# A two-layer decoder trunk on one core: the order of scores, softmax and the product with values in differential attention is changed

## The chip, the core and the metric

The kernel runs on one core of a Trainium2 chip. Its time is the device time of one execution in microseconds. A core has five engines that work side by side, each through its own queue in the order written: TensorE (PE; its weight loads are PEld) multiplies, VectorE (DVE) and ScalarE (ACT) do the element-wise work, GpSimd (POOL) does some of it and issues some DMAs, SyncE (SP) issues most DMAs. An instruction waits at the head of its queue until what it needs has been signalled; everything behind it in that queue waits too.

## The reference

Two layers on x of 512 x 1024 (float32). Layer 0 mixes tokens by causal multi-scale pooling, layer 1 by causal differential attention; each is followed by a SwiGLU FFN, and after each of the four parts stands a LayerNorm on `ALPHA * x + part(x)`. The change lies in the attention of layer 1:

```python
q, k, v = split(x @ w_qkv)              # 8 heads; q, k: 2 components of 64; v: 128 wide
for qb in range(4):                     # blocks of 128 query rows
    s = q[:, :, :, q0:kend] . k[:, :, :, :kend] * sm_scale
    p = softmax(where(rel >= 0, s + bias, -inf))
    a = p[:, :, 0] - lam * p[:, :, 1]
    o = a . v[:, :, :kend]
o = o * rsqrt(mean(o * o) + LN_EPS) * subln_g * (1 - lambda_init)
return concat(o) @ w_o
```

## The kernel before

All products are made at nearly float32 precision from pairs of a high and a low half: `split` (line 116) makes the high half by a cast on ACT and the low half by a subtraction on DVE (or on POOL, where `low` says so), and `mm3` (147) adds three matmuls, high by high, high by low and low by high. A 128 x 512 matmul result is one of eight banks, which are handed out in turn as they come free.

Weights come in rows of 128 x 1024 from one array, `wall`. `fetch` loads a row through SP into one of five raw buffers; `ready(upto)` (126) divides rows up to that number into one of six pairs of buffers, and so its place in the program is the place of that work in the queues of ACT and DVE. Rows in the set `by_dma` (105) are divided in another way: ACT writes the high half and a negated copy, and a DMA that POOL issues adds the row itself to the negated high half while it loads it a second time from memory. In attention the rows are counted from `attn`: rows 0 to 7 are for values and head 0's q and k, rows 8 and 9 q and k of head 1 (in the trace the tiles w76 and w77), 10 and 11 the last part of the values (w78, w79), 12 to 23 q and k of heads 2 to 7 (w80 to w91), and from 24 on the rows of `w_o` (w92 to w99).

The order of every queue is the order in which the program is written (`manual_schedule`, 282). `attention` (1000) first makes the values by a Strassen-like scheme with seven products, whose last but one (Q5) goes to two banks named vc; the last (Q3) is added to them in head 1. Then it goes through the heads (loop at 1330). In turn h stand:

- `combine(h - 1, 3)`, `split_values(h - 1)` (vh on ACT, vl on DVE), in turns 1 to 4 an `affine` of the residual (two passes of DVE), and the load of the next bias
- q of head h (24 matmuls), its division, `root(h - 2)` (two matmuls named ss that sum the squares of the head before the last over 128 rows, then a logarithm and an exponential on ACT), k of head h (24 matmuls), `scaled(h - 2)` (a product on DVE, a cast on ACT, a subtraction on DVE), and the division of k; between them `ready` for coming rows
- `transposed(h - 1)`: ten transposes of the combined map of the head before and its division into ah and al (three casts, three subtractions)
- `score_block(h, q)` for the four blocks of query rows: twelve, pairwise concurrent, half-height matmuls for two components, then per component on DVE the addition of the bias with the minimum in one pass (line 1149) and on ACT the exponential with its sum (1154)
- `combine(h, q)` (1159): three operations of DVE that join the two components of a block; blocks 0, 1 and 2 stand behind softmax blocks 1, 2 and 3, block 3 in the next turn
- `mix(h - 1)` (1188), behind block 3: the product o of the values with the map of the head before (twelve matmuls), its square on ACT (1203), and the division of the square into sqh (ACT) and sql (POOL; in the last head DVE)

Behind the loop `gather` multiplies by the rows of `w_o`, in two parts of four heads. Between the third and the fourth row of its first step stands `root` of head 6, later `transposed`, `mix` and `root` of head 7. In turn 7 `ready` divides w92 and w93 around q and k, w94 behind the transposes and w95 behind score block 0.

Of the kernel before, what the change touches and what calls it, by code (L numbers as in the profile page):

```python
# [16 lines left out]
ALU = mybir.AluOpType  # L17

P = 128
# [7 lines left out]
HEADS = 8  # L27
# [27 lines left out]
def trunk(ctx, tc, x, wall, pscale, lam_p, subln, table, lng, lnb, band, first, onehot, out):  # L55
# [38 lines left out]
    attn = 2 + 3 * FB  # L94
# [7 lines left out]
    rows_of_wall = list(range(total))  # L102
    rows_of_wall[attn : attn + 24] = order_of_rows
    added = {attn + 6 + r: vrow[1] + r for r in range(2)}
    by_dma = {attn + c for c in (8, 9, *range(12, 24))}

    def fetch(upto):
        while fetched[0] < min(upto, total):
# [891 lines left out]
    def attention():  # L1000
        n = 2
        with tc.tile_pool(name="attn", bufs=1) as ap:
# [55 lines left out]
            where = [base[0]]  # L1058
# [3 lines left out]
                where[0] += count  # L1062
                return [weights(c + i) for i in range(count)]

            vs, qk, soft, outs, mid, biases = {}, {}, {}, {}, {}, {}

            def values(p, r, accs, w):
                wh, wl = w
# [14 lines left out]
            def part(half, side, s):  # L1083
                return vals[:, 2 * half + s, side * 512 : (side + 1) * 512]
# [46 lines left out]
                w1 = ap.tile([P, 4], F32, tag="w1", name=f"w1_{h}", bufs=2)  # L1131
                mid[h] = (mn, sm, w1)

            def score_block(h, q):
                (qh, ql), (kh, kl) = qk[h, "q"], qk[h, "k"]
                mn, sm, _ = mid[h]
                w = (q + 1) * P
                wide = max(w, 256)
                accs = [bank(f"s{h}_{q}_{c}") for c in range(2)]
                qs = slice(q * P, (q + 1) * P)  # L1140
                for i, (a, b) in enumerate(((qh, kh), (qh, kl), (ql, kh))):
                    for c in range(2):
                        r = slice(c * HD, (c + 1) * HD)
                        nc.tensor.matmul(  # L1144
                            accs[c][:, :wide], a[r, qs], b[r, :wide], start=i == 0, stop=i == 2
                        )
                for c in range(2):
                    p = soft[h][c][:, OFF[q] : OFF[q] + w]
                    nc.vector.tensor_tensor_reduce(  # L1149
                        out=p, in0=accs[c][:, :w], in1=biases[h][:, w - 1 :: -1] if w < S else biases[h][:, ::-1],  # L1150
                        op0=ALU.add, op1=ALU.min, scale=1.0, scalar=3.0e38,
                        accum_out=mn[:, q, c : c + 1],
                    )
                    nc.scalar.activation(  # L1154
                        p, p, AF.Exp, bias=mn[:, q, c : c + 1], scale=-1.0,
                        accum_out=sm[:, q, c : c + 1],
                    )
# [96 lines left out]
            def combined(t, a, b, op):  # L1254
                nc.vector.tensor_tensor(t, a, b, op=op)
# [9 lines left out]
            w = take(2)  # L1265
# [7 lines left out]
            w = take(2)  # L1273
# [9 lines left out]
            w = take(2)  # L1283
# [37 lines left out]
            ready(where[0] + 2)  # L1321
            for r in range(2):
                values("Q5", r, vc, w[r])
            for s in range(2):
                combined(part(1, 1, s), vc[s], part(1, 1, s), ALU.subtract)
            ah, al = (ap.tile([P, AW], F32R, tag=t, name=t) for t in ("ah", "al"))
            for t in (ah, al):
                nc.gpsimd.memset(t[:, :P].bitcast(F32), 0.0)

            for h in range(HEADS):  # L1330
                if h > 0:
                    combine(h - 1, 3)
                if h > 0:
                    split_values(h - 1)
                if h == 0:
                    scalars()
                if 0 < h <= SB:
                    affine(n - 1, h - 1)
                if h == SB + 1:
                    load_gb(n)  # L1340
                if h + 1 < HEADS:
                    load_bias(h + 1)
                if h > 0:
                    accs = [bank(f"{nm}{h}") for nm in "qk"]
                    w = take(2)
                    ready(where[0] + (3 if h == 1 else 1))
                    query(accs[0], w[0])
                    split_query(h, "q", accs[0])
                    if h > 1:
                        root(h - 2)  # L1350
                    query(accs[1], w[1])
                    ready(where[0] + (4 if h == 1 else 2))
                    if h > 1:
                        scaled(h - 2)
                    split_query(h, "k", accs[1])
                    if h == 1:
                        w = take(2)
                        for r in range(2):
                            values("Q3", r, vc, w[r])
                        for s in range(2):  # L1360
                            combined(part(0, 1, s), vc[s], part(0, 1, s), ALU.subtract)
                    transposed(h - 1)
                if h == HEADS - 1:
                    ready(where[0] + 3)
                start_scores(h)
                score_block(h, 0)
                if h == HEADS - 1:
                    ready(where[0] + 4)
                score_block(h, 1)
                combine(h, 0)  # L1370
                score_block(h, 2)
                combine(h, 1)
                score_block(h, 3)
                if h > 0:
                    mix(h - 1)
                combine(h, 2)
            cw = where[0]
            combine(HEADS - 1, 3)
            split_values(HEADS - 1)
            ws = take(4)  # L1380
            last = HEADS - 1
            between = [
                lambda: root(last - 1), lambda: transposed(last), lambda: mix(last),
                lambda: root(last),
# [137 lines left out]
```

## Time and profile before

| | |
|---|---|
| three runs | 960.09, 962.82, 961.61 us; median 961.61 |
| the profiled execution | 961.99 us, of which the profile's span is 960.1 |
| attention, from the values to the end of `gather` | about 395 to 615 us of the span |
| a turn of the head loop, from the first ss of one head to the next | 18.0 us (454.32 to 472.29) |
| granted PE clock over the span | 0.992 |

In the profile a row of a timeline gives start, duration, engine, line, operation, output and inputs with their shapes, and in brackets the idle time of the engine ahead of it and what ended it. A matmul of 512 columns is shown with about 0.39 us, but matmuls overlap: the distance of two starts counts, about 0.23 us. In a list of waits stand the engine that waited, for whom, the sum in us, the number of times and the longest. A list of stretches gives for each its length, then for PE, PEld, DVE, ACT and POOL the busy time and the instructions, then the granted clock, the busy share of the DMA engines and GB/s.

### The profile page before, as it was taken

Reading aid. Unit: us, or ns where it says so; the run is one execution under the profiler, and the core shown is the slowest. Engines: PE = TensorE matmul, PEld = TensorE weight load, DVE = VectorE, ACT = ScalarE, POOL = GpSimd, SP = SyncE. Lnnn points to the kernel's source line nnn. Section 1 sums busy time; section 2 is a strip of 40 time slices with the busy share of each in tenths; the row PEclk is TensorE's granted clock in tenths of the full one; section 3 lists DMA queues with packets and bytes.
Section 4 is the critical chain, followed back from the end, with each engine's and each line's share of the span. In section 5 each row is a group of like instructions: output and inputs, shape, how many; then the busy total and the mean of one; then the engine's idle time right before and its main releaser. Section 6 shows DMA issues by size and latency. Waiting matters only on the chain.

```text
span 960.1 us, 14943 instructions
## 1 busy us (share of the span) xinstructions
PE 937.1 (98%) x5712; PEld 831.1 (87%) x5712; DVE 793.0 (83%) x1157; ACT 516.3 (54%) x820; POOL 130.2 (14%) x153
## 2 busy tenths in 40 slices
PE   9999999999999999999999979999999999999996
PEld 8898899999988878878777768898899999988885
DVE  8859889999987588877897775879779999988778
ACT  6752445554664278675778753743335555564450
POOL 4121121110002101001212100221211110001101
PEclk9999999999999999999999989999999999999998
DMA  9386988886868996785665522297888886878942
GB/s 245 129 272 211 339 287 251 255 277 201 257 204 283 347 307 191 175 219 143 143 164 132 129 69 83 73 313 213 286 260 245 260 244 215 255 253 277 359 163 89
DMA packets 86182, 211.63 MB, mean 220 GB/s; under 512 B 15156, under 2 KB 26676, under 8 KB 86110
## 3 DMA queue, kind: packets, MB, share of 16 engines
q1 hardware_dynamic: 43420, 117.16, 37.2%
q0 software_dynamic: 18912, 58.73, 24.4%
q10 hardware_dynamic: 23778, 34.78, 10.0%
q8 instruction: 45, 0.74, 0.3%
q14 instruction: 27, 0.22, 0.1%
HBM read 173.93 MB, written 36.72 MB: 219 GB/s over the span
## 4 chain that ended last, share of the span: by engine, by line
PE 71%; issue 10%; DVE 9%; ACT 4%; DMA 3%; POOL 2%; DVEq 0%; ACTq 0%; POOLq 0%
PE A L861 17%; PE P L928 9%; PE C L861 8%; PE B L861 4%; PE Q L928 3%; PE g L151 3%; PE u L151 3%; PE u L150 3%; PE u L149 3%; PE g L150 3%; PE g L149 3%; PE va L1076 2%; DMA r<-tsum 1%; DMA r<-in_wall 1%; PE wo L149 1%
## 5 line engine op out<-in xcount | busy, mean ns | idle before, releaser
L607 DVE TENSOR_TENSOR raw<-raw,raw 128x1024 f32<-128x1024 f32 x56 | 68.3, 1219 | 0.5
L123 ACT CAST xs<-hid 128x512 fp32r<-128x512 f32 (+1 forms) x60 | 34.7, 581 | 24.3 <-DVE hid L775 24.3
L1154 ACT ACTIVATE p<-p,mn 128x128 f32<-128x128 f32 (+3 forms) x64 | 35.4, 554 | 21.6 <-DVE mn L1149 21.6
L124 DVE TENSOR_TENSOR xs<-hid,xs 128x512 fp32r<-128x512 f32 (+1 forms) x60 | 38.4, 641 | 7.8 <-ACT xs L123 7.8
L249 ACT ACTIVATE y<-pt,bT,gT 128x128 f32<-128x128 f32 x80 | 30.1, 456 | 19.4 <-PE pt L235 19.3
L706 POOL DMA_DIRECT2D b<-in_wall x20 | 14.0, 707 | 171.8 <-DMA tsum<-b 118.1
L767 POOL DMA_DIRECT2D xs<-ssum x24 | 17.5, 727 | 140.4 <-PE Q L928 67.4
L199 POOL TENSOR_TENSOR rs<-rs,mhalf 128x1 f32<-128x1 f32 x16 | 12.6, 787 | 153.8 <-DVE rs L198 114.3
L639 DVE TENSOR_TENSOR hid<-sg,u 128x512 f32<-128x512 f32 x16 | 11.0, 686 | 26.1 <-PE u L151 14.1
L706 POOL DMA_DIRECT2D hid<-in_wall x24 | 18.8, 824 | 82.9 <-DMA tsum<-hid 43.9
L743 ACT CAST v<-u 128x512 fp32r<-128x512 f32 x22 | 13.6, 620 | 27.3 <-DVE u L741 27.2
L1149 DVE CUSTOM_DVE_ANT_0 p<-s,bias 128x128 f32<-128x128 f32 (+3 forms) x64 | 28.1, 484 | 0.0
L124 POOL TENSOR_TENSOR sql<-sq,sqh 128x512 fp32r<-128x512 f32 x7 | 11.7, 1675 | 91.5 <-ACT sqh L123 91.5
L124 DVE TENSOR_TENSOR xt<-y,xt 128x512 fp32r<-128x512 f32 x20 | 13.6, 690 | 12.1 <-ACT xt L123 12.1
L190 DVE BATCH_NORM_STATS2 st<-res 128x6 f32<-128x512 f32 x32 | 22.2, 694 | 1.1
L887 ACT ACTIVATE sg<-sg 128x512 f32<-128x512 f32 x14 | 8.9, 633 | 25.7 <-DVE sg L880 25.7
L707 POOL DMA_DIRECT2D hid<-in_wall x12 | 14.8, 1234 | 53.7 <-DMA hid<-in_wall 47.0
L655 ACT CAST xs<-hid 128x1024 fp32r<-128x1024 f32 x8 | 8.4, 1052 | 24.0 <-DVE hid L672 11.6
L1144 PE MATMUL s<-heads 64*128 64x256 f32 (+2 forms) x168 | 19.9, 349 | 0.0
L876 DVE TENSOR_TENSOR hid<-C,hid 128x512 f32<-128x512 f32 x14 | 9.7, 691 | 10.9 <-PE C L861 9.3
L1168 DVE SCALAR_TENSOR_TENSOR p<-p,sm,p 128x128 f32<-128x128 f32 (+3 forms) x32 | 17.6, 551 | 1.1
L872 ACT COPY hid<-C 128x512 f32<-128x512 f32 x14 | 8.2, 588 | 18.5 <-PE C L861 18.5
(1188 smaller groups left out, 3686.4 us busy)
## 6 DMA issues: line engine op xcount, KB each, us to landing
raw<-in_wall SPq DMA_DIRECT2D x122, 512.0 KB, 4.8
r<-tsum SPq DMA_DIRECT2D x40, 512.0 KB, 4.4
hid<-in_wall POOLq DMA_DIRECT2D x36, 512.0 KB, 6.9
b<-in_wall POOLq DMA_DIRECT2D x30, 512.0 KB, 5.7
r<-in_wall SPq DMA_DIRECT2D x30, 512.0 KB, 4.8
tsum<-hid ACTq DMA_DIRECT2D x24, 512.0 KB, 5.7
ssum<-v ACTq DMA_DIRECT2D x22, 512.0 KB, 3.8
tsum<-b ACTq DMA_DIRECT2D x20, 512.0 KB, 4.8
```

The source lines that it names most:

```text
L123: nc.scalar.copy(dst_h, src)
L124: (low or nc.vector).tensor_tensor(dst_l, src, dst_h.bitcast(F32), op=ALU.subtract)
L149: nc.tensor.matmul(acc, ah, bh, start=start, stop=False)
L150: nc.tensor.matmul(acc, ah, bl, start=False, stop=False)
L151: nc.tensor.matmul(acc, al, bh, start=False, stop=stop)
L249: nc.scalar.activation(y[:, k, :], pt[:, k * P : (k + 1) * P], AF.Identity, bias=bT[:, n, kk : kk + 1], scale=gT[:, n, kk : kk + 1],)
L607: tt(t, raws[pair[0]], raws[pair[1]], op=ALU.add)
L706: nc.gpsimd.dma_start(out=t[:, j], in_=src[:, j])
L861: nc.tensor.matmul(o, w[:, c], x[:, kk, :], start=p in ("P1", "Q5", "P2") and f + kk + e == 0, stop=p in ("Q4", "Q3", "P2") and (f, kk, e) ...
L928: nc.tensor.matmul(accs[s], x[:, k, r], y[:, c], start=first and k == 0 and e == 0, stop=last and k == m - 1 and e == 2, skip_group_check= ...
L1149: nc.vector.tensor_tensor_reduce(out=p, in0=accs[c][:, :w], in1=biases[h][:, w - 1 :: -1] if w < S else biases[h][:, ::-1], op0=ALU.add, o ...
L1154: nc.scalar.activation(p, p, AF.Exp, bias=mn[:, q, c : c + 1], scale=-1.0, accum_out=sm[:, q, c : c + 1],)
```

## The change

- `score_block` is cut in two. `scores` holds the twelve matmuls, with the product of q's low half ahead of that of k's low half; `softmax` holds the work of DVE and ACT.
- In each turn blocks 0 and 1 stay as they are. Then come the scores of blocks 2 and 3, then `mix(h - 1)`, and only then, alternating with `combine` of blocks 0 and 1, softmax blocks 2 and 3. For PE the order of matmuls stays the same (except within a score block), as does DVE's order in turns 1 to 6; on ACT the square and the cast of `mix` now stand ahead of the exponentials of blocks 2 and 3.
- In turn 0 the two subtractions of vc (DVE) move from ahead of the first softmax block to behind the second.
- Row 8 (w76, q of head 1) leaves `by_dma`: DVE makes its low half.
- In turn 7 `ready` divides w92 and w93 ahead of q, and w94 and w95 behind k's matmuls, ahead of `scaled` and the division of k.

```diff
-    by_dma = {attn + c for c in (8, 9, *range(12, 24))}
+    by_dma = {attn + c for c in (9, *range(12, 24))}
...
-            def score_block(h, q):
+            def scores(h, q):
                 (qh, ql), (kh, kl) = qk[h, "q"], qk[h, "k"]
-                mn, sm, _ = mid[h]
-                w = (q + 1) * P
-                wide = max(w, 256)
+                wide = max((q + 1) * P, 256)
                 accs = [bank(f"s{h}_{q}_{c}") for c in range(2)]
                 qs = slice(q * P, (q + 1) * P)
-                for i, (a, b) in enumerate(((qh, kh), (qh, kl), (ql, kh))):
+                for i, (a, b) in enumerate(((qh, kh), (ql, kh), (qh, kl))):
                     for c in range(2):
...
+                maps[h, q] = accs
+
+            def softmax(h, q):
+                mn, sm, _ = mid[h]
+                w = (q + 1) * P
+                accs = maps.pop((h, q))
                 for c in range(2):
                     p = soft[h][c][:, OFF[q] : OFF[q] + w]
...
                 values("Q5", r, vc, w[r])
-            for s in range(2):
-                combined(part(1, 1, s), vc[s], part(1, 1, s), ALU.subtract)
...
+            last = HEADS - 1
             for h in range(HEADS):
...
-                    ready(where[0] + (3 if h == 1 else 1))
+                    ready(where[0] + {1: 3, last: 2}.get(h, 1))
                     query(accs[0], w[0])
...
                     query(accs[1], w[1])
-                    ready(where[0] + (4 if h == 1 else 2))
+                    ready(where[0] + (4 if h in (1, last) else 2))
...
-                if h == HEADS - 1:
-                    ready(where[0] + 3)
                 start_scores(h)
-                score_block(h, 0)
-                if h == HEADS - 1:
-                    ready(where[0] + 4)
-                score_block(h, 1)
-                combine(h, 0)
-                score_block(h, 2)
-                combine(h, 1)
-                score_block(h, 3)
+                for q in range(2):
+                    scores(h, q)
+                    softmax(h, q)
+                if h == 0:
+                    for s in range(2):
+                        combined(part(1, 1, s), vc[s], part(1, 1, s), ALU.subtract)
+                for q in (2, 3):
+                    scores(h, q)
                 if h > 0:
                     mix(h - 1)
+                for q in (2, 3):
+                    combine(h, q - 2)
+                    softmax(h, q)
                 combine(h, 2)
```

More of the change, by code (lines that the diff above doesn't have):

```diff
@@ L1063, in take @@
                 return [weights(c + i) for i in range(count)]
-            vs, qk, soft, outs, mid, biases = {}, {}, {}, {}, {}, {}
+            vs, qk, soft, outs, mid, biases, maps = {}, {}, {}, {}, {}, {}, {}
             def values(p, r, accs, w):
@@ L1380, in attention @@
             ws = take(4)
-            last = HEADS - 1
             between = [
```

## The prediction

> **What bounds the kernel now.** I read the page's first part, then busy time in stretches, then the list of waits between 395 and 600 us (the attention layer), and last the timelines of the engines around the waits that PE shows.
>
> ```profile
> PE 937.1 (98%) x5712; PEld 831.1 (87%) x5712; DVE 793.0 (83%) x1157; ACT 516.3 (54%) x820; POOL 130.2 (14%) x153
> ```
> ```profile
> 415.00:444.00 29.00, 27.23 (x130) 21.59 (x128) 17.61 (x45) 18.22 (x33) 3.79 (x6) 0.94 0.87 230
> 560.00:590.00 30.00, 25.46 (x109) 20.40 (x108) 17.22 (x33) 12.36 (x25) 1.66 (x1) 0.89 0.15 52
> 620.00:700.00 80.00, 80.00 (x434) 69.69 (x433) 64.53 (x73) 33.09 (x45) 15.61 (x18) 1.00 0.86 270
> ```
> ```profile
> PEld ss L1211 <- POOL sql L124: 6.2, 7, 1.5
> PE ss L1211 <- POOL sql L124: 3.1, 7, 0.9
> PE ss L1210 <- ACT sqh L123: 3.6, 1, 3.6
> ```
>
> PE is the bound: 98% busy, and 80.00 of 80 us in the FFN behind the attention layer. So time that PE loses inside the attention layer is lost at the end, and time won there arrives at the end. The stretches (after length: PE, PEld, DVE, ACT, POOL, then granted clock) show two places where PE idles and the clock falls: 415 to 444 (0.94) and 560 to 590 (4.5 us idle, 0.89). The waits name the second and a third: `root`'s two matmuls (ss) wait for the squares of seven heads. What sits in the first stands in part 3.
>
> **The change, part by part.**
>
> *1. The last `root` that stands behind softmax.* Timelines of PE, ACT and POOL at the last head:
>
> ```profile
> 557.52 0.28 PE L151 MATMUL o<-ah,vl 128*128 128x256 f32 x1
> 561.51 0.39 PE L151 MATMUL wo<-w94h,heads 128*128 128x512 f32 x1
> 565.49 0.79 PE L1210 MATMUL ss<-sqh,ones 128*128 128x512 f32 x1 [3.59 <-ACT sqh L123]
> 567.24 0.79 PE L1211 MATMUL ss<-sql,ones 128*128 128x512 f32 x1 [0.95 <-POOL sql L124]
> 567.83 0.63 PE L149 MATMUL wo<-w95h,heads 128*128 128x512 f32 x1
> 572.06 0.41 PE L150 MATMUL wo<-w93l,heads 128*128 128x512 f32 x1
> ```
> ```profile
> 564.22 0.57 ACT L1203 ACTIVATE sq<-o 128x512 f32<-128x512 f32 x1
> 564.82 0.62 ACT L123 CAST sqh<-sq 128x512 fp32r<-128x512 f32 x1
> ```
>
> The product o of head 6 is complete at 557.52 + 0.28 = 557.80, but ACT squares it at 564.22, because `mix` stands in its queue behind the exponentials of blocks 1 to 3, and these wait for DVE. Without a wait ss would follow the matmul of 561.51 at 561.74. From there to 572.06, where the pitch is normal again, PE issues 2 ss and 10 wo matmuls: 12 x 0.23 = 2.7 us at full clock (0.23 is the pitch of head 1's k in part 3: 24 matmuls in 5.44 us), against 10.32 us. **7.6 us** are lost, about 5 of them idle and the rest in matmuls at a pitch of 0.43.
>
> With `mix` queued ahead of softmax blocks 2 and 3, ACT squares at once: 0.6 + 0.6 us puts sqh at 559.0, and POOL's 1.68 us puts sql at 560.8. PE comes for it at 561.7: cover of about 1 us, so the whole 7.6 us goes if o does not start later than now (part 4). If sql is late by more than 1 us, the excess comes back one to one. What is late next? `transposed` of head 7 needs the last `combine`. PE would reach it at 561.74 + 26 x 0.23 = 567.7. The last exponential ends today before the square of 564.22, `combine` within 2 us of it, and both come earlier, since the splits of w94 and w95 leave the softmax. It holds.
>
> *2. The six earlier roots* (heads 2 to 7, roots 0 to 5). First and last of six:
>
> ```profile
> 448.69 0.28 PE L151 MATMUL o<-ah,vl 128*128 128x256 f32 x1
> 454.32 0.39 PE L1210 MATMUL ss<-sqh,ones 128*128 128x512 f32 x1
> 455.02 0.50 PE L1211 MATMUL ss<-sql,ones 128*128 128x512 f32 x1 [0.31 <-POOL sql L124]
> 455.36 0.39 PE L149 MATMUL k<-xt,w81h 128*128 128x512 f32 x1
> ...
> 544.49 0.39 PE L1210 MATMUL ss<-sqh,ones 128*128 128x512 f32 x1
> 545.27 0.50 PE L1211 MATMUL ss<-sql,ones 128*128 128x512 f32 x1 [0.39 <-POOL sql L124]
> ```
> ```profile
> 448.41 0.62 ACT L1154 ACTIVATE p<-p,mn 128x384 f32<-128x384 f32 x1 [0.49 <-DVE mn L1149]
> 451.97 0.58 ACT L1203 ACTIVATE sq<-o 128x512 f32<-128x512 f32 x1
> ```
> ```profile
> 453.29 1.68 POOL L124 TENSOR_TENSOR sql<-sq,sqh 128x512 fp32r<-128x512 f32 x1 [17.17 <-ACT sqh L123]
> ```
> ```profile
> 429.94 0.68 DVE L124 TENSOR_TENSOR vl<-vals,vh 128x512 fp32r<-128x512 f32 x1
> ...
> 453.76 1.75 DVE L124 TENSOR_TENSOR vl<-vals,vh 128x512 fp32r<-128x512 f32 x1
> ```
>
> ss to k takes 1.04 us in the first, against 0.46 for two matmuls: 0.6. In the last the second ss comes 0.78 us behind the first, not 0.70: the same or a little more. With `mix` in front, o ends at 448.97, sqh is there at about 450.2 and sql at 451.9, 2.4 us ahead of 454.32. The price lies on ACT and DVE: the exponential of block 2 starts at 450.2 instead of 448.41, block 3's ends at about 452.9 (0.8 later), and `combine` of blocks 2 and 3 ends about 0.7 us later. Two things pay it back. ACT has its squares behind it, so vh starts when it does now. And `vl` stops colliding: it takes 1.75 us where POOL works on sql and 0.68 where it does not. So DVE leaves vl about 0.4 us earlier than today, and no split of q or k is later. Bounds of what the earlier sql can do to DVE are zero and the 1.07 us of that collision, now in `combine`; I take 0.5 and it does not reach PE. Counted: five heads x 0.6 = **3.1 us**; the sixth (head 7) is spent in part 4.
>
> [...]
>
> Scores now take the q low half second and the k low half third. The waits give 1.2 us over six heads to the k low half today. I count nothing (bounds 0 and 1.2): behind the k split DVE still owes three splits of the transposed map before it releases the banks for block 3 and o, and that chain starts no earlier.
>
> *3. Head 0 and head 1.*
>
> ```profile
> 419.03 0.69 DVE L1255 TENSOR_TENSOR vals<-vc,vals 128x512 f32<-128x512 f32 x1 [5.54 <-PE vc L1076]
> 432.94 1.22 DVE L124 TENSOR_TENSOR w78l<-raw,w78h 128x1024 fp32r<-128x1024 f32 x1
> ```
> ```profile
> 422.29 0.70 PE L1144 MATMUL s<-ksq,qsqh 64*128 64x512 f32 x2 [0.51 <-DVE mn L1149]
> 423.39 0.50 PE L149 MATMUL q<-xt,w76h 128*128 128x512 f32 x1
> 425.39 0.79 PE L151 MATMUL q<-xt,w76l 128*128 128x512 f32 x1 [1.26 <-DMA w76l<-in_wall]
> 432.05 0.39 PE L149 MATMUL k<-xt,w77h 128*128 128x512 f32 x1
> 437.49 0.39 PE L1076 MATMUL vc<-w78h,heads 128*128 128x512 f32 x1
> ```
> ```profile
> 425.00:430.00 5.00, 4.61 (x14) 3.67 (x15) 4.78 (x16) 4.17 (x11) 0.00 (x0) 0.66 0.83 181
> ```
> ```profile
> w81l<-in_wall POOLq DMA_DIRECT2D x1, 512.0 KB, 9.5
> ```
>
> q takes 423.39 to 432.05 = 8.66 us, k with the same 24 matmuls 5.44: 3.2 us go to the wait for w76l's landing and to the halved clock behind it (0.66 over 5 us is 1.7 us). With a 1.22 us split on VectorE, in the 5.54 us in which it waits for vc, w76l is there at about 417.7. ACT saves its negated copy (1.06), so w77l's DMA starts 1 us earlier; even with w81l's landing, 9.5 us, the longest in this stretch, it lands about a quarter microsecond before k needs it at 428.3. The two subtractions from vc (2 x 0.69) leave the place ahead of softmax block 0, which then starts about 1 us earlier; block 3 of the scores loses its wait (0.7 us with the restart). They come back behind block 1, so softmax block 2 and everything DVE does after it are 0.2 us later than now. That is the next wait: w78l, done now at 432.94 + 1.22 = 434.16, then at 434.4, while PE reaches it at 433.5. A new stall of 0.9 us. Sum: 3.2 + 0.7 - 0.9 = **3.0 us**.
>
> *4. The wo rows of head 7.*
>
> ```profile
> 549.27 0.75 DVE L1219 SCALAR_TENSOR_TENSOR rso<-o,gcol,rso 128x512 f32<-128x512 f32 x1
> 554.06 1.22 DVE L124 TENSOR_TENSOR w94l<-raw,w94h 128x1024 fp32r<-128x1024 f32 x1
> ```
> ```profile
> 551.24 0.59 ACT L123 CAST heads<-k 128x512 fp32r<-128x512 f32 x1 [0.57 <-PE k L151]
> ```
> ```profile
> 555.64 0.47 PE L149 MATMUL o<-ah,vh 128*128 128x512 f32 x1 [0.55 <-DVE mn L1149]
> ```
>
> w94 and w95 (two casts on ACT, two DVE splits of 1.22) now stand ahead of `scaled`; behind `scaled`'s product wait ACT's cast of it and, in the same queue, the cast of k. Two splits more on DVE (2.4), less what it gains at vl and in idle time (about 1.0), put the product at about 550.7 (549.27 today) and k's cast at 551.9 (551.24), although PE ends k 0.65 us earlier. From k's cast to o the chain loses w94l (1.22 at 554.06), so o starts at 555.5 to 555.6: as now. The head's own 0.6 us is spent, nothing else; PE's idle time moves ahead of the scores. POOL and SP gain no entries there: the raw rows of w92 to w95 are loaded long before.
>
> **Sum**: 7.6 + 3.1 + 3.0 = 13.7 us. The profiled execution took 961.99, so 948.3; the median of the runs is 0.38 lower: **947.9 us**.
>
> **The rivals.** *A stall stays at one of the two halved places.* In head 7 PE idles about 0.9 us ahead of the scores and 1 within them, no less than the two waits (0.51 and 1.26) after which the clock halved in head 1; or w77l lands later than 9.5 us. Either returns 1.7 to 3.2 us: 949.6 to 951.1. For it: both margins are a few tenths. Against: o waits 0.55 us today behind like gaps, and the clock held there.
>
> [...]
>
> *Hidden anyway.* Something behind attention (the first weights of the FFN) ends last, and the gain is given back: about 961.6. Against it: 80.00 of 80 us busy.
>
> [...]
>
> **How the numbers follow.** Forecast 0.67 (945.0 to 949.6: w78l's stall may not come, 0.9, and the k halves may give 1.2, or a lock costs 1 to 1.5); a stall stays 0.22; hidden 0.07; slower 0.04. The range 945.0 to 952.0 holds the first two. This kernel's measurement tells 0.3% (2.9 us) from no change: faster 0.90, within 0.06, slower 0.04.
>
> **What would show it.** Right: in the list of waits ss no longer waits for sqh or sql; the PE timeline runs without a gap from o of head 6 to `root`; the clock column reads 1.00 between 560 and 590 and about 425; q of head 1 takes 5.5 us; a wait of vc for w78l appears. Wrong: PE waiting for the k split in every head, DVE's `combine` stretched by more than 1 us, or a halved window inside head 7.

## The result and the profile after

| | before | after |
|---|---|---|
| runs, us | 960.09, 962.82, 961.61, 961.51 | 948.47, 948.79, 948.29, 950.59 |
| median, us | 961.56 | 948.63 |
| span of the profiled execution, us | 960.1 | 946.7 |
| granted PE clock over the span | 0.992 | 0.997 |

The ratio is 0.987 with an interval of 0.9851 to 0.989. The forecast was 947.9 us, with a range of 945.0 to 952.0: the time lies 0.7 us above the forecast.

The busy times of the changed kernel, from the first part of its page:

```profile
PE 931.2 (98%) x5712; PEld 829.9 (88%) x5712; DVE 787.3 (83%) x1158; ACT 513.8 (54%) x819; POOL 126.5 (13%) x152
```

PE has the same 5712 matmuls and was busy 5.9 us less (937.1 before). So more than half of the 13.4 us by which the span became shorter was idle time of PE, and the rest lay in matmuls that took longer before, many of them under the halved clock: six of q of head 1 and nine of wo took 0.63 us each at a granted clock of 0.50, against 0.39 and 0.40 in the changed kernel at 1.00. The stretches of the changed kernel say where:

```profile
415.00:444.00 29.00, 28.54 (x157) 22.76 (x156) 21.45 (x59) 19.26 (x39) 2.94 (x5) 1.00 0.77 211
547.00:577.00 30.00, 29.82 (x152) 24.86 (x153) 19.64 (x47) 15.19 (x34) 1.29 (x1) 1.00 0.15 52
```

Both places where PE idled are full, and the clock is 1.00 in both (before: 0.94 and 0.89; the second place has moved forward by 13 us). All waits of PE in the attention of the changed kernel (395 to 600 us):

```profile
PE s L1142 <- ACT heads L123: 0.8, 1, 0.8
PE vc L1076 <- DVE w78l L124: 0.5, 1, 0.5
PE s L1142 <- DVE heads L124: 0.3, 1, 0.3
```

The waits of ss for the squares are gone. What is new was forecast: the wait for w78l, and in head 7 two waits of the scores for k.

To count by stage, one reads when PE starts the same matmul in both traces. The start of the first transpose behind attention (pt) and the first scores of heads 0, 1 and 6, before:

```profile
420.28 0.39 PE L1144 MATMUL s<-ksq,qsqh 64*128 64x256 f32 x2
...
444.12 0.39 PE L1144 MATMUL s<-heads 64*128 64x256 f32 x2
...
534.21 0.38 PE L1144 MATMUL s<-heads 64*128 64x256 f32 x2
...
602.22 0.44 PE L235 MATMUL pt<-ident,res 128*128 128x128 f32 x2
```

The same in the changed kernel, with the first o of head 6 ahead of pt:

```profile
420.40 0.39 PE L1142 MATMUL s<-ksq,qsqh 64*128 64x256 f32 x2
...
440.94 0.39 PE L1142 MATMUL s<-heads 64*128 64x256 f32 x2
...
528.05 0.39 PE L1142 MATMUL s<-heads 64*128 64x256 f32 x2
...
549.59 0.51 PE L149 MATMUL o<-ah,vh 128*128 128x512 f32 x1
...
588.62 0.44 PE L235 MATMUL pt<-ident,res 128*128 128x128 f32 x2
```

| stage | won, us | forecast, us |
|---|---|---|
| up to the scores of head 0 | -0.12 | 0 |
| heads 0 and 1, to the scores of head 1 | (444.12 - 420.28) - (440.94 - 420.40) = 3.30 | 3.0 |
| five heads, to the scores of head 6 | (534.21 - 444.12) - (528.05 - 440.94) = 2.98 | 3.1 |
| head 7, to o of head 6 | (555.64 - 534.21) - (549.59 - 528.05) = -0.11 | 0 |
| from there to pt, with the last root | (602.22 - 555.64) - (588.62 - 549.59) = 7.55 | 7.6 |
| sum | 13.60 | 13.7 |

At the end of the span 13.4 of the 13.6 us are left.

### The profile page after: what moved, and what is told of

The parts are those of the page before. It is cut to its first block, busy times and chain, and to the rows that moved or that the text cites. A ratio compares the mean times of both kernels' runs of the same rounds, so it can differ in the third digit from the quotient of the medians.

```text
span 946.7 us, 14942 instructions
## 1 busy us (share of the span) xinstructions
PE 931.2 (98%) x5712; PEld 829.9 (88%) x5712; DVE 787.3 (83%) x1158; ACT 513.8 (54%) x819; POOL 126.5 (13%) x152
## 4 chain that ended last, share of the span: by engine, by line
PE 82%; DVE 9%; ACT 3%; DMA 3%; issue 2%; POOL 0%; DVEq 0%; ACTq 0%; POOLq 0%
PE A L861 17%; PE P L928 9%; PE C L861 9%; PE B L861 4%; PE Q L928 3%; PE g L151 3%; PE u L149 3%; PE u L150 3%; PE u L151 3%; PE g L149 3%; PE g L150 3%; PE va L1076 2%; PE s L1142 2%; DMA r<-tsum 1%; DMA r<-in_wall 1%
## 5 line engine op out<-in xcount | busy, mean ns | idle before, releaser
L743 ACT CAST v<-u 128x512 fp32r<-128x512 f32 x22 | 13.6, 620 | 27.7 <-DVE u L741 27.7
L124 DVE TENSOR_TENSOR xt<-y,xt 128x512 fp32r<-128x512 f32 x20 | 13.6, 690 | 12.1 <-ACT xt L123 12.1
L1142 PEld LDWEIGHTS s<-heads 64*128 64x128 f32 x168 | 14.1, 185 | 5.2 <-issue 1.0
L876 DVE TENSOR_TENSOR hid<-C,hid 128x512 f32<-128x512 f32 x14 | 9.7, 691 | 10.4 <-PE C L861 8.8
```

Of the source, the lines that this page charges most:

```text
L124: (low or nc.vector).tensor_tensor(dst_l, src, dst_h.bitcast(F32), op=ALU.subtract)
L1142: nc.tensor.matmul(accs[c][:, :wide], a[r, qs], b[r, :wide], start=i == 0, stop=i == 2)
```

## The experiments

All kernels here compute the whole reference. "The changed kernel" is the base of each diff, except where the text says otherwise.

The runs were made in several sets, and the median of the kernel before lay between 960.50 and 961.98 us from set to set, so medians of different kernels compare to about 1 us. Therefore the text also counts one stretch in each trace, "scores to pt": from the first scores of head 0 to the first transpose behind attention. It is 602.22 - 420.28 = 181.94 us before and 588.62 - 420.40 = 168.22 in the changed kernel. The scores of head 0 start anywhere from 419.25 to 421.59 us in the thirteen traces, though PE's program up to there is the same in all; the medians hold this scatter, the stretch does not. There is one trace of each kernel.

### Undoing the early squares: e1_squares_last

```diff
                 for q in (2, 3):
                     scores(h, q)
-                if h > 0:
-                    mix(h - 1)
                 for q in (2, 3):
                     combine(h, q - 2)
                     softmax(h, q)
+                if h > 0:
+                    mix(h - 1)
                 combine(h, 2)
```

> The changed kernel, but the product with values and its squares stand behind softmax block 3 again in every turn; all scores still stand ahead, the wo rows, row 8 and the vc subtractions stay as changed. My theory: the wait of ss for sql comes back in heads 2 to 6, 0.6 us each (3.0 us); in head 7 it is absorbed by the late k cast. In the last head sql comes about 8.2 us behind the start of o, PE is there after 6.1: about 2.2 us of wait, and 1.7 us more if the clock halves. So 953.8 us, up to 955.5. Rival A (the order of the squares is worth the whole of parts 1 and 2, the moved wo rows nothing): 948.6 + 10.6 = 959.2. Rival B (the gain came from all scores being queued ahead, not from the squares): 948.6 to 949.5, and no wait of ss in the list.

Measured: 953.99 us (952.87 to 957.13), ratio 0.9936 [0.991, 0.9961]. PE's waits in the attention:

```profile
PE ss L1215 <- POOL sql L124: 3.3, 7, 1.2
```

The last of the seven in the PE timeline:

```profile
560.23 0.50 PE L1214 MATMUL ss<-sqh,ones 128*128 128x512 f32 x1 [0.16 <-ACT sqh L123]
561.97 0.50 PE L1215 MATMUL ss<-sql,ones 128*128 128x512 f32 x1 [1.24 <-POOL sql L124]
```

With the squares behind the exponentials again, PE waits for sql in all seven heads again, and 953.99 - 948.63 = 5.4 of the 10.7 us of parts 1 and 2 are lost (scores to pt: 173.46, 5.2 more than the changed kernel). The last root, however, now costs 1.9 us and not 7.6 (from 559.68 to 562.31 it is 2.63 us for three distances of 0.23: the two waits of 0.16 and 1.24 us and 0.5 us of restarts around them): the rows of `w_o` still stand ahead of head 7's softmax, so the square is late by little. Without early squares the rest of the change thus gives back 5.7 of the 7.6 us. That it is the moved rows is argued, not isolated: they are what the rest changes on DVE and ACT in the last head. That the early squares alone give back nearly all of it is shown by the next two runs.

### Undoing the moved rows of `w_o`: e2_wo_rows_back

```diff
-                    ready(where[0] + {1: 3, last: 2}.get(h, 1))
+                    ready(where[0] + (3 if h == 1 else 1))
...
-                    ready(where[0] + (4 if h in (1, last) else 2))
+                    ready(where[0] + (4 if h == 1 else 2))
...
+                if h == last:
+                    ready(where[0] + 3)
                 start_scores(h)
                 for q in range(2):
+                    if h == last and q == 1:
+                        ready(where[0] + 4)
                     scores(h, q)
```

> The changed kernel, but in head 7 the wo rows are divided in the old places (w94 behind the transposes, w95 between softmax blocks 0 and 1). My theory: k's cast is early again, o starts about 0.6 us earlier than in the changed kernel, w94l and w95l push softmax blocks 0 and 1, so sql comes 0.5 us too late for PE: these cancel, 948.2 to 949.3, with a wait of ss for sql of 0.3 to 0.8 us in the last head and no gap of 1 us ahead of head 7's scores. Rival (most of the last head's 7.6 us came from taking w95 out of the softmax): 951 to 954, with a wait of several us at ss.

Measured: 948.74 us (948.57 to 949.55), ratio 0.9877 [0.986, 0.9895], against 948.63 for the changed kernel. The waits in its attention:

```profile
PE o L149 <- DVE mn L1153: 0.6, 1, 0.6
...
PE ss L1215 <- POOL sql L124: 0.4, 1, 0.4
```

The idle time ahead of head 7's scores is gone; o waits for the softmax as it did before the change, and the last ss waits 0.4 us for sql. It is the same sum in other places (scores to pt: 168.20): beside the early squares the moved rows are worth nothing.

### The early squares alone: e5_squares_alone

The kernel before, with `score_block` cut in two and `mix` ahead of softmax blocks 2 and 3 as in the change; the product of k's low half stays second, and rows 8, w94, w95 and the subtractions of vc stay where they were.

> The kernel before with one part of the change alone: all scores, then the product with values and its squares, then softmax blocks 2 and 3. wo rows, row 8, the vc subtractions and the order of the low halves stay as before. My theory: 3.0 us in heads 2 to 6 and about 7.4 in head 7 and the last root, although w95 still stands in the softmax: 961.6 - 10.4 = 951.2 us. Rival A (the last head needs the wo rows moved too): 955 or more, with a wait of several us at the last ss. Rival B (softmax held up by the squares makes the k split late, which only the other parts hid): 954 or more with PE waiting ahead of the scores in each head.

Measured: 950.82 us (950.52 to 953.37), ratio 0.9906 [0.9881, 0.9931]. By the medians this part carries 10.7 of the 12.9 us. By the trace, against the kernel before, it won 3.0 us in the five heads, 0.6 in head 7 and 6.8 behind it, 10.4 us in all; 1.6 us more were won in heads 0 and 1, which this edit should leave as they were. That is the surprise of this profile: PE waits there and then the stretch from 424 to 434.

```profile
422.74 0.70 PE L1142 MATMUL s<-ksq,qsqh 64*128 64x512 f32 x2 [0.51 <-DVE mn L1153]
425.75 0.50 PE L151 MATMUL q<-xt,w76l 128*128 128x512 f32 x1 [1.17 <-DMA w76l<-in_wall]
```
```profile
424.00:434.00 10.00, 8.83 (x38) 6.96 (x39) 9.71 (x23) 8.67 (x19) 0.64 (x1) 1.00 0.69 168
```

Nearly the same two waits as before (0.51 and 1.26 there), but the granted clock stays at 1.00. The same stretch of the kernel before:

```profile
424.00:434.00 10.00, 8.74 (x32) 6.98 (x32) 9.75 (x22) 8.68 (x18) 0.85 (x1) 0.83 0.66 166
```

So the 1.7 us that part 3 of the prediction puts down to the halved clock at head 1 do not follow from these waits with certainty; in one execution they come, in another not. Before, the clock was halved from 425.23 to 428.64, for 3.41 us, and nearly the whole of both waits lies in the 3.41 us just ahead of that:

```profile
421.82:425.23 3.41, 1.83 (x8) 0.98 (x8) 3.25 (x19) 2.47 (x10) 0.00 (x0) 1.00 1.02 201
425.23:428.64 3.41, 3.25 (x8) 2.58 (x9) 3.30 (x10) 2.58 (x9) 0.00 (x0) 0.50 0.77 192
```

PE was without a matmul for 3.41 - 1.83 = 1.58 us of the first. In e5's trace the two waits add up to 1.68 us, against 1.77 before. Why the clock halved behind the one pair and not behind the other was not shown.

### Undoing the row on VectorE: e3_row8_by_dma and e7_row8_dma_bias_late

```diff
-    by_dma = {attn + c for c in (9, *range(12, 24))}
+    by_dma = {attn + c for c in (8, 9, *range(12, 24))}
```

> The changed kernel, but the low half of head 1's q comes by DMA again. My theory: it lands at about 425.4 us, PE needs it at 423.1: 2.3 us of wait in q of head 1, with 1.7 us more if the clock halves, less the 0.7 us that head 1 now waits for w78l and then no longer does: 950.2 to 951.9 us. Rival (the landing cost little by itself; what won the 3.3 us in heads 0 and 1 was the moved vc subtractions): 948.6 to 949.4.

Measured: 953.99 us (953.75 to 956.12), ratio 0.9935 [0.9915, 0.9956]. That is above the whole expected range: the edit costs 5.4 us (scores to pt: 173.33, 5.1 more). The wait of PE, the landing of w76l and the stretch from 427 on:

```profile
427.26 0.50 PE L151 MATMUL q<-xt,w76l 128*128 128x512 f32 x1 [3.78 <-DMA w76l<-in_wall]
```
```profile
w76l<-in_wall POOLq DMA_DIRECT2D x1, 512.0 KB, 9.2
```
```profile
427.00:432.00 5.00, 4.74 (x14) 3.75 (x15) 4.86 (x12) 4.82 (x9) 0.00 (x0) 0.66 0.71 202
```

Theory and rival had taken w76l's landing from before, 7.6 us. It took 9.2. What had changed beside it is in the SP timelines: the load of head 1's bias, here and (second fence) in the kernel before.

```profile
418.08 0.42 SPq L1117 DMA_DIRECT2D bias<-lines  x1
```
```profile
421.51 0.33 SPq L1117 DMA_DIRECT2D bias<-lines  x1
```

With the subtractions of vc out of the way, the first four small operations of `scalars` run 7.4 us earlier on DVE (from 413.64 here, from 421.00 before); they release a buffer, SP's queue goes on, and the bias is loaded 3.4 us earlier, issued 0.1 us behind w76l (417.97). To test it, the same kernel with that load issued later:

```diff
-                if h + 1 < HEADS:
+                if 1 < h + 1 < HEADS and h != 1:
                     load_bias(h + 1)
...
                     ready(where[0] + {1: 3, last: 2}.get(h, 1))
+                    if h == 1:
+                        load_bias(1)
+                        load_bias(2)
```

> The kernel with row 8 by DMA (e3), but head 1's bias is loaded after the next raw rows instead of as soon as its buffer is free. New theory for the 9.2 us landing of w76l in e3: the moved vc subtractions let the scalars of the lambda term run 3 us earlier, which frees the bias buffer, so that the bias load (issued at 418.1 instead of 421.9) shares the DMA engines with w76l. Then the landing goes back to 7.5 us, the wait in q to about 2.3 us: 952.3 us, or 950.6 where the clock does not halve. [...]

Measured: 952.77 us (951.78 to 954.57), ratio 0.9912 [0.9894, 0.993].

```profile
426.53 0.50 PE L151 MATMUL q<-xt,w76l 128*128 128x512 f32 x1 [2.48 <-DMA w76l<-in_wall]
```
```profile
w76l<-in_wall POOLq DMA_DIRECT2D x1, 512.0 KB, 7.9
```

The landing falls from 9.2 to 7.9 us and the wait from 3.8 to 2.5 (scores to pt: 171.82, 1.5 less than e3), while DVE does the same work in the same order beside it; so the loads made the difference, as far as one landing in each trace can show. The edit moved more than one load: both biases are now issued from 436.22 on, and the next raw row of 512 KB, which stood behind them in SP's queue, came forward from 428.20 to 420.16. That row, 1.6 us behind w76l's issue, may be the 0.3 us left over 7.6; no run here tests it. In these traces the order of DVE's work thus changed, by way of SP's queue, how long a transfer took that DVE neither issues nor reads.

### Undoing the move of the subtractions: e4_vc_back

```diff
+            for s in range(2):
+                combined(part(1, 1, s), vc[s], part(1, 1, s), ALU.subtract)
             ah, al = (...)
...
-                if h == 0:
-                    for s in range(2):
-                        combined(part(1, 1, s), vc[s], part(1, 1, s), ALU.subtract)
```

> The changed kernel, but the two subtractions of vc stand ahead of head 0's first softmax again. My theory: the fourth score block of head 0 waits 0.7 us for its bank again and q of head 1 starts about 0.9 us later; in return PE no longer waits for w78l (0.7 us). The two cancel: 948.7 to 949.1 us. Rival (the moved subtractions win their 0.7 us by themselves, w78l would wait anyway): 949.5 us, with both waits in the trace.

Measured: 948.09 us (947.52 to 948.46), ratio 0.9861 [0.9844, 0.9878]. In its trace the wait for w78l is gone and the wait of the scores for the softmax is back:

```profile
421.83 0.70 PE L1142 MATMUL s<-ksq,qsqh 64*128 64x512 f32 x2 [0.51 <-DVE mn L1153]
```

The move wins about 0.7 us in head 0 and gives it back in head 1. As expected it cancels (scores to pt: 168.40, against 168.22); the run is even 0.5 us below the changed kernel, which these measurements do not tell apart.

### The order within a score block: e6_k_low_second

```diff
-                for i, (a, b) in enumerate(((qh, kh), (ql, kh), (qh, kl))):
+                for i, (a, b) in enumerate(((qh, kh), (qh, kl), (ql, kh))):
```

> The changed kernel, but k's low half is multiplied second again in every score block. My theory: scores to o stays 2.79 us in heads 2 to 6, since block 3 and o wait for the banks that the splits of the transposed map release; 948.6 us, within 0.3. Rival (the third place hides the k split, 0.2 us in each of six heads): 949.8 us and 2.9 to 3.0 us from scores to o.

Measured: 948.23 us (947.79 to 948.82), ratio 0.9863 [0.9849, 0.9878]. By the distances of starts PE again loses 0.26 us per head at k's low half, yet a turn, from the first scores of head 2 to those of head 3, stays at 17.41 us (458.36 to 475.77; in the changed kernel 458.25 to 475.66). What the new order spares at k's low half is lost again before o: from the first scores to o it is 2.80 us here and 2.79 in the changed kernel. That is what the expectation said; that the wait is for banks, as it also said, was not tested. The prediction counted nothing for this edit.

### Better orders: v3_mix_before_scores, v4_affine_in_gaps, v2_order_mended, v5_casts_behind_k

If PE needs an early square, the product with values could stand ahead of all scores. For that the transposes go into the middle of k:

```diff
-                if 0 < h <= SB:
-                    affine(n - 1, h - 1)
...
-                    query(accs[1], w[1])
-                    ready(where[0] + (4 if h in (1, last) else 2))
+                    query(accs[1], w[1], range(KB // 2))
+                    ready(where[0] + (4 if h == 1 else 2))
                     if h > 1:
                         scaled(h - 2)
+                    transposed(h - 1)
+                    if h == last:
+                        ready(where[0] + 3)
+                    if h <= SB:
+                        affine(n - 1, h - 1)
+                    query(accs[1], w[1], range(KB // 2, KB))
                     split_query(h, "k", accs[1])
...
-                    transposed(h - 1)
+                    mix(h - 1)
                 start_scores(h)
...
+                if h == last:
+                    ready(where[0] + 4)
...
-                if h > 0:
-                    mix(h - 1)
```

> A version made from what the traces show to be left: the transposes of the head before stand in the middle of k's matmuls and the product with values directly behind k, ahead of all scores; the affine of the residual stands behind the transposes' splits; in the last head w94 is divided behind the transposes and w95 behind softmax block 1. If the waits left in the scores (for the k split and for the banks of the transposed map) are what costs 0.6 us a head, they go: 7 x 0.6, with 0.7 for w78l and 1.5 in the last head 942.2 us, and PE shows no wait for VectorE or ScalarE between 440 and 545. Rival (VectorE's chain of combine, splits and affine is the next bound, since the transposes now come 5 us earlier): PE waits for combine ahead of the transposes or for the split map ahead of o, 946 us or more.

Measured: 949.0 us (948.34 to 950.69), ratio 0.9874 [0.9856, 0.9891]: a miss, nothing was won over the changed kernel (scores to pt: 169.25, 1.0 more). PE's waits, then DVE around the third of the four:

```profile
PE s L1142 <- DVE heads L124: 4.9, 4, 1.5
```
```profile
492.84 1.61 DVE L124 TENSOR_TENSOR al<-at,ah 128x512 fp32r<-128x512 f32 x3
494.37 1.22 DVE L227 TENSOR_TENSOR res<-res,gb 128x1024 f32<-128x1024 f32 x1
495.62 1.23 DVE L228 TENSOR_TENSOR res<-res,gb 128x1024 f32<-128x1024 f32 x1
496.77 0.68 DVE L124 TENSOR_TENSOR heads<-k,heads 128x512 fp32r<-128x512 f32 x1
```

I had put `affine`, which nobody waits for, between al and the low half of k, for which PE waits. It has 2.45 us in heads 2 to 4, and PE loses 1.7 us in each. The next kernel puts its two halves into gaps of DVE: the first inside `scaled`, ahead of the division, the second behind k's low half (`times` and `plus` are the two lines of `affine`; the base is v3).

```diff
                 nc.vector.scalar_tensor_tensor(rs, acc, gcol, rs, op0=ALU.mult, op1=ALU.mult)
+                if h < SB - 1:
+                    times(n - 1, h + 1)
...
-                    if h <= SB:
-                        affine(n - 1, h - 1)
+                    if h == 1:
+                        affine(n - 1, 0)
...
                     split_query(h, "k", accs[1])
+                    if 1 < h <= SB:
+                        plus(n - 1, h - 1)
```

> The kernel of the last variant (the product with values ahead of the scores), with one thing moved: in turns 2 to 4 the two halves of `affine` (1.22 and 1.23 us on VectorE) no longer stand together ahead of the low half of k. The first stands inside `scaled`, where VectorE waited 1.65 us for the cast of the high half; the second stands behind the low half of k, where VectorE waited about 1.1 us for the first scores in heads 5 to 7. Theory: the order on VectorE alone made TensorE wait 1.68 to 1.70 us ahead of the scores of heads 2, 3 and 4. Then these three gaps go, 3 x 1.69 = 5.1 us, and the run gives 949.0 - 5.1 = 943.9 us (943.2 to 944.8). Rival: the low half of k was late because VectorE's whole turn had become too long, wherever `affine` stands; then the gap is only shared out, at least 1 us per head stays, and the run gives 947 us or more.

Measured: 945.38 us (944.61 to 947.51), ratio 0.9831 [0.98, 0.9861]. The three gaps went. The time is 0.6 us above the expected range, and the waits of PE say why:

```profile
PE o L150 <- DVE al L124: 0.6, 4, 0.2
...
```

Heads 2 to 4 of v3 lost their time ahead of the scores, behind o; now the next heads come to o earlier and wait about 0.3 us (with the restart) for al, as the later heads of v3 did. That gives back 1.0 of the 5.1 us: scores to pt fell by 4.1, to 165.13. The last 0.5 us is within what these runs scatter (2.9 us).

The other way is to leave the change's order and move two pieces: the division of w95 behind softmax block 1 of head 7 (w94 stays ahead of `scaled`; the expectation describes this edit wrongly), and `affine` to just ahead of q's division (in head 1 behind it):

```diff
-                if 0 < h <= SB:
-                    affine(n - 1, h - 1)
...
+                    if 1 < h <= SB:
+                        affine(n - 1, h - 1)
                     split_query(h, "q", accs[0])
+                    if h == 1:
+                        affine(n - 1, 0)
...
-                    ready(where[0] + (4 if h in (1, last) else 2))
+                    ready(where[0] + {1: 4, last: 3}.get(h, 2))
...
+                if h == last:
+                    ready(where[0] + 4)
```

> The changed kernel with three orders altered: the low half of the second row of weights of head 7 behind k instead of ahead of it and the next row's behind softmax block 1 (the PE idle of 0.97 us ahead of head 7's scores should go), `affine` of row 0 behind the split of q in head 1, and `affine` ahead of the split of q in heads 2 to 4. Theory: the idle ahead of head 7's scores (0.97 + 0.50 us) is VectorE's queue, so 1.0 to 1.5 us go, and of head 1's stall (0.62 + 0.11 us) most: 948.6 - 1.0 - 0.6 = 947.0 us (946.3 to 947.8). Rival: the idle only moves to the next wait of the same engine, and the time stays within 0.3% of the changed kernel, 948.1 to 949.1 us.

Measured: 945.76 us (945.34 to 946.13), ratio 0.9827 [0.9803, 0.9851], 0.5 us below the expected range. By the trace the two moves won 2.0 us (scores to pt: 166.22), 0.75 in heads 0 and 1 and 1.1 in head 7, against 1.6 expected; another 1.15 us of its trace lie ahead of the scores of head 0, where nothing was edited. Its list of waits of PE has no entry between 420 and 600 us.

The last kernel is v4 with `ready` for the second row of weights moved behind the division of k:

```diff
-                    ready(where[0] + (4 if h == 1 else 2))
+                    if h == 1:
+                        ready(where[0] + 4)
...
-                    if h == last:
-                        ready(where[0] + 3)
...
                     split_query(h, "k", accs[1])
+                    if h > 1:
+                        ready(where[0] + (3 if h == last else 2))
```

> The kernel of v4_affine_in_gaps with the two casts of the second row of weights (1.03 and 1.06 us on ScalarE) moved from ahead of `scaled` to behind the split of k in turns 2 to 7. Theory: the waits that are left, 0.27 to 0.32 us for the low half of the transposed maps (al) ahead of each product with values from head 1 to head 6, and 0.51 us for k of head 7, come from these casts, behind which ScalarE's cast to ah stands; behind k ScalarE had 1.71 us of idle. Then 5 x 0.32 + 0.27 + 0.51 = 2.4 us go less what the casts now delay: 945.4 - 2.4 = 943.0 us (942.3 to 943.9). Rival: the two casts (2.1 us) are longer than the idle that they fill and delay the square and the exps by 0.4 us, VectorE comes late with al in the turn behind, and the time stays at 945 us or more.

Measured: 945.45 us (944.13 to 945.65), ratio 0.9827 [0.9811, 0.9843], no difference from v4. The waits for al went in all heads but one, but the casts that stand later also issue their DMA later, and one of these is late, that of turn 4 for k of head 5 (issued at 493.12 against 489.65 in v4, and landed 8.8 us after its issue, in v4 7.0):

```profile
PE k L151 <- DMA w87l<-in_wall: 0.9, 1, 0.9
```

The rival named ScalarE's exponentials as what is late next; it was a transfer. v2, v4 and v5 lie within 0.4 us of each other, about 3 us below the changed kernel; the medians do not tell the three apart. The stretch from scores to pt orders them (166.22, 165.13 and 164.59), by one trace of each.

## Why the prediction was right, point by point

**What bounds the kernel.** Right. Time won by PE in attention arrived at the end: 13.6 us at the first transpose behind attention, 13.4 at the end.

**Part 1, the last root.** Right in size (7.55 against 7.6) and in mechanism. In the changed kernel, PE around the last ss of head 6:

```profile
555.49 0.40 PE L151 MATMUL wo<-w94h,heads 128*128 128x512 f32 x1
555.72 0.39 PE L1214 MATMUL ss<-sqh,ones 128*128 128x512 f32 x1
...
558.49 0.39 PE L150 MATMUL wo<-w93l,heads 128*128 128x512 f32 x1
```

From the matmul ahead of ss (555.49; 561.51 before) to the one that stood at 572.06 before (558.49) it takes 3.00 us, against 10.55. ACT squares as soon as o is complete:

```profile
551.89 0.60 ACT L1207 ACTIVATE sq<-o 128x512 f32<-128x512 f32 x1 [1.13 <-PE o L151]
```

By the tile view sql starts at 553.2 on POOL, so with 1.29 us it ends at 554.5, 1.5 us ahead of its ss (555.96). One thing the prediction did not say: it named the moved rows of `w_o` only as help for the transposes, while e1, which keeps them and has late squares, gives back 5.7 of the 7.6 us; and in e2, beside the early squares, they are worth nothing.

**Part 2, the earlier roots.** The gain was 2.98 us against 3.1, and sql is there long before ss. Not right was the place of the collision. The prediction let sql meet `combine` and took 0.5 us for it. In the groups of the changed kernel, POOL and DVE:

```profile
L124 POOL TENSOR_TENSOR sql<-sq,sqh 128x512 fp32r<-128x512 f32 x7 | 9.1, 1294 | 67.0 <-ACT sqh L123 67.0
```
```profile
L124 DVE TENSOR_TENSOR vl<-vals,vh 128x512 fp32r<-128x512 f32 x8 | 5.5, 684 | 0.0
...
L1172 DVE SCALAR_TENSOR_TENSOR p<-p,sm,p 128x384 f32<-128x384 f32 x8 | 4.9, 618 | 0.3
```

vl now takes 0.68 us in all eight heads and `combine`'s second operation 0.618, as before: nothing collides. The timeline of head 2 shows why.

```profile
447.15 1.30 POOL L124 TENSOR_TENSOR sql<-sq,sqh 128x512 fp32r<-128x512 f32 x1 [10.85 <-ACT sqh L123]
```
```profile
447.25 0.69 DVE L1153 CUSTOM_DVE_ANT_0 p<-s,bias 128x512 f32<-128x512 f32 x1
...
448.31 0.17 DVE L1167 RECIPROCAL sm<-sm 128x2 f32<-128x2 f32 x1 [0.36 <-ACT p L1158]
448.51 0.48 DVE L1168 TENSOR_SCALAR p<-p,sm,nlam 128x384 f32<-128x384 f32 x1
```

sql runs from 447.15 to 448.45, beside softmax block 3, and is over 0.06 us before `combine` of block 2 starts its first wide operation. The softmax pass takes 0.69 us beside sql, against a mean of 0.684 for the 16 of this width in the kernel before, while vl took 1.75 us beside sql and takes 0.68 alone. What sets the two apart no run here isolates. The kernel before shows `combine` beside sql too, as the one of the two that came first. There its second operation runs just ahead of vl:

```profile
453.06 0.75 DVE L1168 SCALAR_TENSOR_TENSOR p<-p,sm,p 128x512 f32<-128x512 f32 x1
```

sql starts inside it, at 453.29. The operation takes 0.75 us, the same as in the changed kernel, and sql takes 1.68 us instead of 1.29. So sql, which started inside `combine`'s operation, took about 0.4 us longer, and vl, which started inside sql, took 1.07 longer. What sql does to a `combine` that starts behind it was not tried. The lock that the chances count with 1 to 1.5 us is shown by no run; in its place the runs showed vl at 1.75 us beside sql, and in the changed kernel `combine`'s second operation of 128 x 512 at 0.752 us, against 0.751 before.

DVE pays elsewhere, 0.36 to 0.42 us per head in which `combine` waits for the exponential (2.8 us in seven heads); it does not reach PE.

**Part 3, heads 0 and 1.** The changed kernel's q, k and last values:

```profile
422.53 0.51 PE L149 MATMUL q<-xt,w76h 128*128 128x512 f32 x1
...
428.10 0.39 PE L149 MATMUL k<-xt,w77h 128*128 128x512 f32 x1
...
433.54 0.39 PE L1076 MATMUL vc<-w78h,heads 128*128 128x512 f32 x1
434.39 0.50 PE L1076 MATMUL vc<-w78l,heads 128*128 128x512 f32 x1 [0.46 <-DVE w78l L124]
```

q took 5.57 us instead of 8.66: 3.1 won (forecast 3.2). From the first scores to q it was 422.53 - 420.40 = 2.13 against 3.11: 1.0 won (forecast 0.7). The new stall at w78l was 434.39 - 433.54 - 0.23 = 0.62 us, and 0.77 with its restart to the scores of head 1 (12.84 us from k, against 12.07), where the forecast had 0.9. Three small errors that make 0.3 us. w77l landed 8.2 us after its issue at 418.8, at 427.0, 1.5 us ahead of its use, and not a quarter of a microsecond: the forecast had taken the longest landing in sight, 9.5.

What the mechanism lacked: 1.7 of the 3.2 us are a halved clock, and e5 shows like waits without it. The forecast was made against one profiled execution that had it; had that profile been like e5's, part 3 would have come out at 1.3 us, from a time 1.7 us shorter. So the time forecast hangs little on it, the gain does.

**Part 4, the rows of `w_o`.** The net was right (-0.11 against 0), the path also, though the idle time within the scores was half of that forecast:

```profile
546.34 0.51 PE L1142 MATMUL s<-heads 64*128 64x256 f32 x4 [0.75 <-ACT heads L123]
547.18 0.50 PE L1142 MATMUL s<-heads 64*128 64x256 f32 x4 [0.34 <-DVE heads L124]
```

The scores of head 7 waited first for ACT's cast of k and then for DVE's low half, both behind `scaled`: 0.97 and 0.50 us by the distances of starts, against 0.9 and 1 forecast. The clock did not halve (1.00 from 538 to 563), so the first rival did not come: the two listed waits are 1.09 us, against 1.77 us in the two waits of head 1 before. v2 takes this idle time away and gains 1.1 us with it.

**The rivals.** Nothing was hidden: 13.4 of 13.6 us arrive. DVE did not fall behind: the list of waits has no wait for k in heads 2 to 6.

## What to carry to other kernels

When an engine's queue holds a short step of the path behind long steps off it (here two operations of 0.6 us behind three blocks of exponentials), move the short one ahead, and count its gain with everything that stands behind the matmul that waits. Ask of each piece on a busy engine who waits for it: `affine` in front of k's low half cost 1.7 us a head; with the same instructions in gaps, three heads together came out 4.1 us shorter. Before you take a transfer's landing time from an old trace, look at what loads beside it in the new order: here earlier work on one engine released a buffer and moved a load, and another one took 1.3 to 1.6 us longer.

## What the runs showed of the hardware

- The halving of PE's clock did not follow from the waits with certainty. In one stretch, waits of 0.51 and 1.26 us came with a granted clock of 0.83 over 10 us (before) and waits of 0.51 and 1.17 with 1.00 (e5). Before, the clock was halved from 425.23 to 428.64 (3.41 us), was full for 136.53 us (40 times 3.41), and was halved from 565.17 to 572.00 (6.83 us, twice 3.41). In e7 it was halved from about 427.2 to 430.6 and in e3 from about 428.5 to 431.9, each again for 3.4 us. In the 3.41 us just ahead of a halving PE stood without a matmul for 1.58 and 3.27 us (before), 2.48 (e7) and 2.19 (e3). No limit comes out of it: in e3 the 3.41 us ahead of those held 1.59 us and were not followed by a halving. In head 7 of the changed kernel waits of 0.75 and 0.34 us came with a clock of 1.00. What decides is not shown.
- POOL's subtraction of 128 x 512 takes 1.29 us beside the softmax pass, against 1.68 in the kernel before (mean of seven each), where it starts inside the second operation of `combine`. That operation keeps its 0.75 us, while vl, which comes behind the subtraction, takes 1.75 us instead of 0.68: what had started first kept its time.
- The landing of one DMA that adds 512 KB (w76l) was 7.5 to 9.2 us in kernels that divide it in the same way, with other loads beside it, and that of w77l was 6.2 us in e4 and 8.2 in the changed kernel.
